# VectorE in written order around the context's last rows, and the second matrix's sums on GpSimd from the third pair on

## The chip, the core and the metric

The kernel runs on one core of a Trainium2 chip. A core has five engines that take their instructions from queues of their own: PE (TensorE, matrix products), DVE (VectorE, element-wise work), ACT (ScalarE, activations and copies), POOL (GpSimd) and SP (SyncE, which here only issues DMAs). They meet through semaphores. The metric is device time in microseconds, the median of repeated executions.

## The reference

One inference step of a layer over 1280 rows of width 1024: 1024 latent rows and 256 context rows. All of it is float32. The part that matters here is the end of the layer:

```python
x  = x + gt1 * (merged @ w_out)
u2 = rmsnorm(x, g_norm2) * (1 + sc2) + sh2
x  = x + gt2 * (jnp.square(jax.nn.relu(u2 @ w_ff1)) @ w_ff2)
y  = rmsnorm(x, g_final)
```

`w_ff1` has 4096 columns and `w_ff2` 4096 rows. The scales and shifts differ between latent and context rows.

## The kernel before

The rows lie in ten tiles of 128 rows, `xt[0..9]`, in one large buffer `z`. Three groups of rows are named `GROUPS`: two of 512 latent rows (tiles 0 to 3 and 4 to 7) and one of 256 context rows (tiles 8 and 9). Each product of float32 numbers is made of three products of rounded parts: an operand is split into a high part, which ACT rounds, and a low part, which DVE subtracts (`h` and `l` at the end of a tile's name). So each new operand needs an ACT and a DVE instruction before PE can use it all.

**The output projection** (`project_out`, L1140) makes 24 matmuls for each row tile and each block of columns, into a PSUM tile `po`. DVE multiplies it by the gate (L1153) and adds it to the row (L1155); ACT sums the squares of the row's new part into `fsq` (L1156). For the context rows it is called by `context_out(q)` in four quarters of 256 columns; each splits four tiles of weights (`raw_wc`, `hi_wc`, `lo_wc`; L861 to L864).

**The normalisation and transposition** (`modulate_ff(g)`, L1100) reduces `fsq` (L1104), makes the reciprocal root (DVE L129, then POOL L130), scales the rows by quarters of columns (`xn`; even tiles on ACT L1116, odd ones on DVE L1118), transposes them on PE (`pt`, L1124) and applies scale and shift on ACT. For latent groups the result is `u2r`, split into `u2h` and `u2l` (L1136, L1137). For the context it is split in place into `u2c` (L1129, L1130).

**The first feed-forward matrix** works on pairs of 128-column blocks, 16 pairs in all. For the latent rows it uses a scheme with seven block products instead of eight: with the four quarters B11, B12, B21, B22 of `u2` (row sums, L762) come T1 to T4, and from the weights come sums of their own (L929). `Pair.begin` makes the products with B11 and B21, `contexts` those of the context rows with `u2c` (`fc`), `rest` those with T4, T2, T3, T1 and B22 in this order. `split_sum` (L771, L772) splits the T tiles. Each product's weights are split in turn (`a_` and `s_` tiles, L854 and L855). `sums` prepares the left operands of the second matrix and stores them.

**The second matrix's sums** (`second_sums(fp)`): SP loads two 512 KB blocks of `w_ff2` into four buffers of `z` (L1221), POOL makes four subtractions (L1224), and a POOL DMA stores the result to `scr_t` (L1225). There is one set of these buffers, and it is where the context's rows `xt[8]` and `xt[9]` lie until they have been stored and scaled. The later phase that multiplies by `w_ff2` (from L1280 on) reads `scr_t`.

**The order of the work.** The kernel is written with a tile framework. Its scheduler orders each engine's instructions, by a simulated time of its own and by the order in which they are written, so an instruction that is ready early may run ahead of earlier written ones on its engine. A `Pinned` wrapper (L35) takes this freedom away: an instruction that is issued through it stays behind the one written just before it on its engine. In the kernel before, only an early phase is pinned (L258 to L395); here VectorE, GpSimd and SP are not. An engine runs its queue in order, and a waiting instruction holds up those behind it.

Around the change, the text of the kernel before has this order: `modulate_ff(1)`, `context_out(2)`, `context_out(3)`, pairs 0 and 1 `begin`, `modulate_ff(2)`, all row sums, the splits of T4, T3, T2, T1, `contexts` of pairs 0 and 1, then for each pair `rest`, `sums` and its `second_sums`.

Of the kernel before, what the change touches and what calls it, by code (L numbers as in the profile page):

```python
# [10 lines left out]
ALU = mybir.AluOpType  # L11
# [37 lines left out]
def hybrid_step(  # L49
# [6 lines left out]
    nc = tc.nc  # L56
    engines = nc.vector, nc.scalar, nc.gpsimd, nc.tensor
    V, A, G, PE = engines
    SP = nc.sync
# [9 lines left out]
    def slot(name, dt=F32R):  # L69
        return sp.tile([P, 512], dt, tag="s", name=name)  # L70
# [4 lines left out]
    def ps_mm(name):  # L75
        return pp.tile([P, 512], F32, tag="mm", name=name, bufs=3)

    def ps_sd(name):
        return pp.tile([P, 512], F32, tag="sd", name=name, bufs=5)

    def small(shape, name, bufs=4):
        return cp.tile(shape, F32, tag=f"sm{shape[-1]}", name=name, bufs=bufs)
# [44 lines left out]
    def rstd_of(ssq, n, name):  # L127
        r = small([P, 16], f"rs_{name}")
        V.tensor_scalar(r[:, :n], ssq, 1.0 / n_of[name[0]], EPS, ALU.mult, ALU.add)  # L129
        G.tensor_tensor(r[:, :n], r[:, :n], neghalf[:, :n], ALU.pow)  # L130
        return r
# [126 lines left out]
    V, A, G, PE = (Pinned(tc, e) for e in engines)  # L258
# [136 lines left out]
    V, A, G, PE = engines  # L395
# [83 lines left out]
    for g in range(3):  # L479
        t0, n = GROUPS[g]  # L480
# [168 lines left out]
    for q in range(2):  # L649
        wq = [load_w(w_sv[q, hf], f"sv{q}_{hf}", eng=G) for hf in range(2)]  # L650
        for i in range(NT):
            g, o = (i * P) // 512, (i * P) % 512
# [18 lines left out]
    def zs(i, n=1):  # L671
        return z[:, i * 512 : (i + n) * 512]
# [82 lines left out]
    def quarter_sums(raw):  # L755
        for kk in range(4):
            b11, b21, b12, b22 = raw["B11"][kk], raw["B21"][kk], raw["B12"][kk], raw["B22"][kk]
            if raw is u_raw:
                for t, k, g in ((b11, kk, 0), (b12, kk, 1), (b22, kk + 4, 1), (b21, kk + 4, 0)):
                    SP.dma_start(t, scr_u[g][k])  # L760
            for out, x, y in ((b11, b12, b11), (b12, b22, b12), (b22, b22, b11), (b21, b22, b21)):
                V.tensor_tensor(out, x, y, ALU.subtract)  # L762

    def split_sum(dst, raw, nm):
        for kk in range(4):
            t = raw[SUMS[nm]][kk]
            if nm == "T2" and kk < 3:
                hi, lo = (six(f"t2{i}{kk}") for i in "hl")
            else:
                hi, lo = slot(f"{nm}h{kk}"), slot(f"{nm}l{kk}")  # L770
            A.copy(hi, t)  # L771
            V.tensor_tensor(lo, t, hi.bitcast(F32), ALU.subtract)  # L772
            dst[nm, kk] = hi, lo
# [69 lines left out]
    def six(name):  # L843
        return q1.tile([P, 512], F32R, tag="th", name=name, bufs=6)
# [4 lines left out]
    def tmp2(name, dt=F32):  # L849
        return q1.tile([P, 512], dt, tag="s", name=name, bufs=6)  # L850
# [156 lines left out]
    for ri, r in enumerate(ORDER):  # L1007
        scr = (scr_ya, scr_yb, scr_yc)[r]
        ys = [[] for _ in range(4)]
        for g in range(3):  # L1010
            for kc in range(4):
                t0, n = GROUPS[g]
# [6 lines left out]
        for d in range(KT):  # L1019
            if d % 2 == 0:  # L1020
                wb = [load_half(w_branch[r, d // 2][:, i * 512 : i * 512 + 512], f"wb{r}_{d}_{i}") for i in range(2)]
            for g in range(3):
                t0, n = GROUPS[g]
# [45 lines left out]
    def context_weights(q):  # L1069

        src = w_out[q // 2][:, :, q % 2 * 256 : q % 2 * 256 + 256].rearrange("(j k) p c -> j p k c", k=2)
        return [load_half(src[i], f"wc{q}_{i}", lambda t: t.rearrange("p (k c) -> p k c", k=2)) for i in range(4)]
# [24 lines left out]

    fsq = cp.tile([P, NT, 4], F32, name="fsq")

    def modulate_ff(g):  # L1100
        t0, n = GROUPS[g]
        tiles = range(t0 // P, (t0 + n) // P)
        fs = small([P, 4], f"fs{g}")[:, : len(tiles)]
        V.reduce_sum(fs, fsq[:, tiles[0] : tiles[-1] + 1, 0 : 4 if g == 2 else 2], axis=mybir.AxisListType.X)  # L1104
        r = rstd_of(fs, len(tiles), f"f{g}")

        j = 1 if g == 2 else 0
        for qt in range(4):
            xn = []
            for ii, i in enumerate(tiles):  # L1110
                if ii % 2 == 0:
                    t = tmp2(f"xn{i}_{qt}")
                v = t[:, (ii % 2) * 256 : (ii % 2) * 256 + 256]
                xv = xt[i][:, qt * 256 : (qt + 1) * 256]
                if ii % 2 == 0:
                    A.activation(v, xv, AF.Copy, scale=r[:, ii : ii + 1])  # L1116
                else:
                    V.tensor_scalar(v, xv, r[:, ii : ii + 1], None, ALU.mult)  # L1118
                xn.append(v)
            for kk in range(2):  # L1120
                k = qt * 2 + kk
                ps = ps_sd(f"pt2{g}_{k}")
                for ii in range(n // P):
                    PE.transpose(ps[:, ii * P : (ii + 1) * P], xn[ii][:, kk * P : (kk + 1) * P], ident)  # L1124
                if g == 2:
                    c = slot(f"u2{k}c")
                    u2c[k] = hi, lo = c[:, 0:256], c[:, 256:512]
                    A.activation(ps[:, :n], ps[:, :n], AF.Identity, bias=sh2[:, k, j : j + 1], scale=a2[:, k, j : j + 1])
                    V.tensor_copy(hi, ps[:, :n])  # L1129
                    V.tensor_tensor(lo, ps[:, :n], hi.bitcast(F32), ALU.subtract)  # L1130
                    continue
                rf = raw2[g][k] = slot(f"u2r{k}_{g}", F32)
                A.activation(rf, ps[:, :n], AF.Identity, bias=sh2[:, k, j : j + 1], scale=a2[:, k, j : j + 1])
                if g == 0 or k >= 4:
                    hi, lo = slot(f"u2h{k}_{g}"), slot(f"u2l{k}_{g}")
                    V.tensor_copy(hi, rf)  # L1136
                    V.tensor_tensor(lo, rf, hi.bitcast(F32), ALU.subtract)  # L1137
                    u2s[f"B{1 + k // 4}{1 + g}", k % 4] = hi, lo

    def project_out(tiles, c0, n, weights):  # L1140

        for i in tiles:
            g = min(i // 4, 2)
            o = i * P - GROUPS[g][0]
            full = ps_mm(f"po{c0}_{i}")
            ps = full[:, :n]
            for k in range(KT):
                whi, wlo = weights(k)
                mh, ml = mT[k][g]
                PE.matmul(ps, mh[:, o : o + P], whi, start=k == 0, stop=False)  # L1150
                PE.matmul(ps, ml[:, o : o + P], whi, start=False, stop=False)  # L1151
                PE.matmul(ps, mh[:, o : o + P], wlo, start=False, stop=k == KT - 1)  # L1152
            V.tensor_tensor(ps, ps, gt1[(2 if g == 2 else 0) + c0 // 512][:, c0 % 512 : c0 % 512 + n], ALU.mult)  # L1153
            xc = xt[i][:, c0 : c0 + n]
            V.tensor_tensor(xc, xc, ps, ALU.add)  # L1155
            A.activation(ps, xc, AF.Square, accum_out=fsq[:, i, c0 // n : c0 // n + 1])  # L1156
            if c0 + n == D:
                SP.dma_start(scr_x[i], xt[i])

    def context_out(q):  # L1160
        ws = context_weights(q)
        project_out((8, 9), q * 256, 256, lambda k: tuple(w[:, k % 2 * 256 : k % 2 * 256 + 256] for w in ws[k // 2]))

    project_out(range(8), 0, 512, lambda k: w_out0[k])
    w_out1 = out_weights(1)
    project_out(range(5), 512, 512, lambda k: w_out1[k])
    modulate_ff(0)
    project_out(range(5, 8), 512, 512, lambda k: w_out1[k])  # L1170
    context_out(0)
    context_out(1)
    modulate_ff(1)
    quarters = (("B11", 0, 0), ("B21", 0, 4), ("B12", 1, 0), ("B22", 1, 4))
    raw2q = {nm: raw2[g][o : o + 4] for nm, g, o in quarters}
    context_out(2)
    context_out(3)

# [36 lines left out]
    def second_sums(fp):  # L1217

        q = [zs(16 + i) for i in range(4)]
        for r in range(2):  # L1220
            SP.dma_start(zs(16 + 2 * r, 2), w_ff2[2 * fp + r])  # L1221
        b11, b12, b21, b22 = q
        for out, x, y in ((b11, b12, b11), (b12, b22, b12), (b22, b22, b11), (b21, b22, b21)):
            G.tensor_tensor(out, x, y, ALU.subtract)  # L1224
        G.dma_start(scr_t[fp], zs(16, 4).rearrange("p (q c) -> p q c", c=512))  # L1225


    pairs = {}

    def feed_pair(fp):  # L1230
        odd = fp % 2
        pairs[fp] = FeedPair(
            f"{fp}", fp, (w_ff1[2 * fp], w_ff1[2 * fp + 1]), 4 if odd else 0, range(8, 12) if odd else range(12, 16), u2s, u2c)

    for fp in (0, 1):
        feed_pair(fp)
        pairs[fp].begin()
    modulate_ff(2)
    quarter_sums(raw2q)
    for nm in ("T4", "T3", "T2", "T1"):  # L1240
        split_sum(u2s, raw2q, nm)
    for fp in (0, 1):
        pairs[fp].contexts()
    for fp in range(NFP):
        if fp not in pairs:
            feed_pair(fp)
            pairs[fp].begin()
            pairs[fp].contexts()
        pairs[fp].rest()
        pairs[fp].sums()  # L1250
        del pairs[fp]
        second_sums(fp)


    pa.close()
# [261 lines left out]
```

## Time and profile before

| | |
|---|---|
| median of 3 runs | 1947.99 us (1946.2 to 1952.21) |
| profiled execution | 1952.31 us, its span 1950.5 us |
| busy share of the span: PE, DVE, ACT, POOL | 98%, 66%, 44%, 20% |
| mean granted TensorE clock | 0.996 |
| longest waits of PE from 1100 to 1260 us | 3.0, 1.5, 0.8 and 0.4 us |

How to read the rows: a row of the timeline has the start, the duration, the engine, the line, the operation, the written and the read tiles (buffer numbers left out, so all buffers of a pool share a name), and, in brackets, how long the engine stood idle before it and what ended that. Merged rows have a count (x4). A row of the windows has the stretch, its length, the busy time and number of instructions of each engine, the granted TensorE clock (1.00 is full speed), the share and rate of the DMA engines. A row of the waits has the waiting instruction, what it waited for, and the sum, number and longest of the waits.

### The profile page before, as it was taken

Reading aid. Unit: us, or ns where it says so; the run is one execution under the profiler, and the core shown is the slowest. Engines: PE = TensorE matmul, PEld = TensorE weight load, DVE = VectorE, ACT = ScalarE, POOL = GpSimd, SP = SyncE. Lnnn points to the kernel's source line nnn. Section 1 sums busy time; section 2 is a strip of 40 time slices with the busy share of each in tenths; the row PEclk is TensorE's granted clock in tenths of the full one; section 3 lists DMA queues with packets and bytes.
Section 4 is the critical chain, followed back from the end, with each engine's and each line's share of the span. In section 5 each row is a group of like instructions: output and inputs, shape, how many; then the busy total and the mean of one; then the engine's idle time right before and its main releaser. Section 6 shows DMA issues by size and latency. Waiting matters only on the chain.

```text
span 1950.5 us, 28164 instructions
## 1 busy us (share of the span) xinstructions
PE 1905.8 (98%) x10160; PEld 1628.3 (83%) x10160; DVE 1295.9 (66%) x2205; ACT 863.2 (44%) x1767; POOL 381.1 (20%) x380
## 2 busy tenths in 40 slices
PE   6999999999999999999999999999999999999998
PEld 3788888998788888888888888888888888888886
DVE  6584443347849889785665489788776655654665
ACT  7443554653233333342123375554454545443443
POOL 1200001117302424230000005445531110000003
PEclk9999999999999999999999999999999999999999
DMA  9111111012534445459533335776773596654444
GB/s 358 76 44 40 48 38 40 27 52 73 191 126 160 153 157 164 136 180 335 166 114 113 141 117 185 278 263 254 265 263 137 190 335 203 208 172 151 166 134 159
DMA packets 148989, 312.71 MB, mean 160 GB/s; under 512 B 17520, under 2 KB 40944, under 8 KB 146800
## 3 DMA queue, kind: packets, MB, share of 16 engines
q1 hardware_dynamic: 107024, 220.10, 33.8%
q0 software_dynamic: 15520, 57.75, 7.8%
q10 hardware_dynamic: 26304, 33.04, 4.7%
q8 instruction: 80, 1.31, 0.3%
q14 instruction: 61, 0.50, 0.1%
HBM read 217.47 MB, written 93.36 MB: 159 GB/s over the span
## 4 chain that ended last, share of the span: by engine, by line
PE 54%; DVE 3%; issue 1%; ACT 0%; DMA 0%; POOL 0%; ACTq 0%; POOLq 0%; DVEq 0%
PE w L1385 6%; PE w L1386 6%; PE w L1387 6%; PE fT L874 3%; PE fT L872 3%; PE fT L873 3%; PE pb L1033 3%; PE pb L1032 3%; PE pb L1034 3%; PE fB L874 2%; PE fB L872 2%; PE fB L873 2%; PE po L1152 2%; PE po L1151 2%; PE po L1150 2%; PE fc L874 1%
## 5 line engine op out<-in xcount | busy, mean ns | idle before, releaser
L1224 POOL TENSOR_TENSOR z<-z 128x512 f32<-128x512 f32 x64 | 101.5, 1586 | 128.0 <-DMA z<-in_w_ff 118.7
L929 DVE TENSOR_TENSOR z<-z 128x512 f32<-128x512 f32 x112 | 94.8, 846 | 2.5
L509 POOL PARTITION_ALL_REDUCE acc<-acc x16 | 55.0, 3472 | 187.8 <-DVE acc L503 101.1
L503 DVE SCALAR_TENSOR_TENSOR acc<-z,scond,acc 128x512 f32<-128x512 f32 x112 | 86.2, 818 | 0.0
L1339 POOL TENSOR_TENSOR rs_y<-rs_y,neghalf 128x1 f32<-128x1 f32 x10 | 9.6, 958 | 334.5 <-DVE rs_y L1338 334.4
L1190 ACT ACTIVATE z<-z 128x512 f32<-128x512 f32 x64 | 40.5, 633 | 69.9 <-DVE z L938 38.4
L954 ACT ACTIVATE z<-z 128x512 f32<-128x512 f32 x48 | 30.4, 633 | 67.8 <-DVE z L938 29.5
L130 POOL TENSOR_TENSOR rs_h<-rs_h,neghalf 128x4 f32<-128x4 f32 (+1 forms) x12 | 10.9, 910 | 202.5 <-DVE rs_h L129 202.3
L1038 DVE TENSOR_TENSOR sg<-pb,sg 128x512 f32<-128x512 f32 (+1 forms) x48 | 28.8, 601 | 26.6 <-PE pb L1034 26.5
L863 ACT CAST hi_wb<-raw_wb 128x512 fp32r<-128x512 f32 x24 | 14.8, 622 | 64.4 <-PE pb L1033 37.2
L635 DVE SCALAR_TENSOR_TENSOR yc<-th,ccol,z 128x512 f32<-128x512 f32 (+1 forms) x12 | 7.9, 660 | 50.4 <-PE th L633 50.4
L1191 ACT ACTIVATE z<-z 128x512 f32<-128x512 f32 x64 | 40.3, 630 | 1.1
L1153 DVE TENSOR_TENSOR po<-po,gt 128x512 f32<-128x512 f32 (+1 forms) x24 | 14.6, 609 | 35.5 <-PE po L1152 35.3
L1215 POOL DMA_DIRECT2D scr_s<-x x48 | 26.4, 551 | 49.5 <-DVE x L1209 44.5
L720 POOL TENSOR_TENSOR z<-z 128x1024 f32<-128x1024 f32 (+13 forms) x20 | 33.6, 1701 | 7.7 <-ACT z L704 5.4
L510 POOL TENSOR_TENSOR acc<-acc,bt 1x512 f32<-1x512 f32 x16 | 24.0, 1515 | 56.4 <-issue 56.4
L1156 ACT ACTIVATE po<-z 128x512 f32<-128x512 f32 (+1 forms) x24 | 12.7, 529 | 48.4 <-DVE z L1155 34.2
L569 DVE SCALAR_TENSOR_TENSOR z<-z,dmb,kv 128x129 f32<-128x129 f32 x56 | 16.3, 345 | 26.2 <-PE kv L558 26.1
L1039 DVE TENSOR_TENSOR z<-z,sg 128x512 f32<-128x512 f32 (+1 forms) x48 | 28.7, 601 | 1.2
L622 DVE TENSOR_TENSOR den<-den,gcol 128x2 f32<-128x2 f32 x40 | 6.3, 160 | 33.5 <-ACT den L621 32.6
L43 PE MATMUL pm<-wah,shl 128*4 128x512 f32 x32 | 13.8, 461 | 13.8 <-ACT wah L43 13.8
L130 POOL TENSOR_TENSOR rs_f<-rs_f,neghalf 128x4 f32<-128x4 f32 (+1 forms) x3 | 3.3, 1093 | 116.9 <-DVE rs_f L129 116.9
(5165 smaller groups left out, 7293.5 us busy)
## 6 DMA issues: line engine op xcount, KB each, us to landing
z<-in_w_ff SPq DMA_DIRECT2D x64, 512.0 KB, 5.4
z<-in_w_ada SPq DMA_DIRECT2D x64, 256.0 KB, 3.2
scr_t<-z POOLq DMA_DIRECT2D x16, 1024.0 KB, 4.9
z<-in_w_in SPq DMA_DIRECT2D x24, 512.0 KB, 4.3
scr_g<-z ACTq DMA_DIRECT2D x48, 256.0 KB, 2.0
sg<-scr_g SPq DMA_DIRECT2D x48, 256.0 KB, 4.6
scr_h<-z ACTq DMA_DIRECT2D x48, 256.0 KB, 4.1
scr_s<-x POOLq DMA_DIRECT2D x48, 256.0 KB, 4.5
```

Source lines behind the costliest of these rows:

```text
L503: V.scalar_tensor_tensor(acc[j], raw, scond[:, k, j : j + 1], acc[j], ALU.mult, ALU.add)
L872: PE.matmul(ps, whi[:, s], ahi, start=first and k == ks[0], stop=False)
L873: PE.matmul(ps, whi[:, s], alo, start=False, stop=False)
L874: PE.matmul(ps, wlo[:, s], ahi, start=False, stop=end and k == ks[-1])
L929: V.tensor_tensor(out, x, y, op)
L1032: PE.matmul(pb[:, :n], whi[:, s], yh, start=kc == 0, stop=False)
L1033: PE.matmul(pb[:, :n], whi[:, s], yl, start=False, stop=False)
L1034: PE.matmul(pb[:, :n], wlo[:, s], yh, start=False, stop=kc == 3)
L1224: G.tensor_tensor(out, x, y, ALU.subtract)
L1385: PE.matmul(banks[j], h_[:, s], rh, start=fp == 0, stop=False)
L1386: PE.matmul(banks[j], l_[:, s], rh, start=False, stop=False)
L1387: PE.matmul(banks[j], h_[:, s], rl, start=False, stop=fp == NFP - 1)
```

## The change

It has three parts.

1. VectorE is pinned from `context_out(2)` to `context_out(3)`, and again from `modulate_ff(2)` to the splits of the T tiles; between the two, `begin` of pairs 0 and 1 is not pinned. The row sums, 16 differences, are cut into four groups of four. One group follows `context_out(2)`; one stands in `context_out(3)` ahead of its last tile's products and addition; one stands in `modulate_ff(2)` between the request of the reciprocal root and the first scaling; one follows `modulate_ff(2)`. T2 is split ahead of T3.
2. The weights of pairs 0 and 1 are requested earlier in the text, ahead of `context_out(2)`.
3. SP is pinned in the loop over the pairs, and `second_sums` are not called for pairs 0 and 1: pair 2 and pair 3 call two each, in order, and from pair 4 on each calls one.

```diff
-    def modulate_ff(g):
+    def modulate_ff(g, between=None):
...
         r = rstd_of(fs, len(tiles), f"f{g}")
+        if between:
+            between()
...
-    def project_out(tiles, c0, n, weights):
+    def project_out(tiles, c0, n, weights, between=None):
 
         for i in tiles:
+            if between and i == tiles[-1]:
+                between()
...
-    context_out(2)
-    context_out(3)
...
     for fp in (0, 1):
         feed_pair(fp)
+
+    def row_sums(kk):
+        b11, b21, b12, b22 = (raw2q[nm][kk] for nm in ("B11", "B21", "B12", "B22"))
+        for out, x, y in ((b11, b12, b11), (b12, b22, b12), (b22, b22, b11), (b21, b22, b21)):
+            V.tensor_tensor(out, x, y, ALU.subtract)
+
+
+    V = Pinned(tc, engines[0])
+    context_out(2)
+    row_sums(0)
+    context_out(3, lambda: row_sums(1))
+    V = engines[0]
+    for fp in (0, 1):
         pairs[fp].begin()
-    modulate_ff(2)
-    quarter_sums(raw2q)
-    for nm in ("T4", "T3", "T2", "T1"):
+    V = Pinned(tc, engines[0])
+
+    modulate_ff(2, lambda: row_sums(2))
+    row_sums(3)
+    for nm in ("T4", "T2", "T3", "T1"):
         split_sum(u2s, raw2q, nm)
+    V = engines[0]
     for fp in (0, 1):
         pairs[fp].contexts()
+    SP = Pinned(tc, nc.sync)
+    summed = 0
     for fp in range(NFP):
...
         pairs[fp].sums()
         del pairs[fp]
-        second_sums(fp)
+
+        for _ in range(min(2, fp + 1 - summed) if fp > 1 else 0):
+            second_sums(summed)
+            summed += 1
+    SP = nc.sync
```

More of the change, by code (lines that the diff above doesn't have):

```diff
@@ L1158, in project_out, with context_out @@
                 SP.dma_start(scr_x[i], xt[i])
-    def context_out(q):
+    def context_out(q, between=None):
         ws = context_weights(q)
-        project_out((8, 9), q * 256, 256, lambda k: tuple(w[:, k % 2 * 256 : k % 2 * 256 + 256] for w in ws[k // 2]))
+        project_out((8, 9), q * 256, 256, lambda k: tuple(w[:, k % 2 * 256 : k % 2 * 256 + 256] for w in ws[k // 2]), between)
     project_out(range(8), 0, 512, lambda k: w_out0[k])
```

## The prediction

> **What bounds the kernel.** I read the page from the top: engines, then TensorE's (PE's) waits in the stretch that the change touches, then that stretch cut into windows, then the engines in order of time.
>
> ```profile
> PE 1905.8 (98%) x10160; PEld 1628.3 (83%) x10160; DVE 1295.9 (66%) x2205; ACT 863.2 (44%) x1767; POOL 381.1 (20%) x380
> ```
>
> TensorE is busy for 98% of the span, so a change elsewhere is worth only the PE time that it takes away or adds. From 1100 to 1260 us, which holds everything the diff touches up to the fourth pair, PE's waits are four:
>
> ```profile
> PE pt L1124 <- ACT xn L1116: 3.0, 1, 3.0
> PE fc L874 <- DVE a_0l L855: 1.5, 1, 1.5
> PE fT L874 <- DVE s_0l L855: 0.8, 1, 0.8
> PE fT L872 <- ACT a_0h L854: 0.4, 1, 0.4
> ```
>
> The windows (length, then PE, weight loads, DVE, ACT, POOL busy; then granted clock) put them in place:
>
> ```profile
> 1138.00:1164.10 26.10, 26.10 (x179) 24.00 (x178) 25.16 (x50) 18.11 (x38) 0.00 (x0) 1.00 0.19 68
> 1164.10:1176.80 12.70, 9.58 (x65) 8.88 (x64) 10.33 (x25) 10.25 (x21) 4.79 (x4) 0.87 0.35 126
> 1176.80:1190.20 13.40, 10.76 (x68) 9.31 (x68) 13.40 (x22) 10.52 (x23) 5.27 (x4) 1.00 0.53 177
> ...
> 1207.00:1560.00 353.00, 353.00 (x1872) 305.40 (x1871) 266.40 (x396) 177.85 (x330) 136.49 (x150) 1.00 0.66 235
> ```
>
> PE is full to 1164.1 and from 1207 on. Idle are 3.12 us (12.70 - 9.58) and 2.64 us (13.40 - 10.76), 5.8 together. Inside the first hole the clock also falls:
>
> ```profile
> 1164.10:1167.20 3.10, 0.14 (x1) 0.00 (x0) 2.11 (x6) 2.26 (x5) 0.70 (x1) 1.00 0.23 88
> 1167.20:1168.50 1.30, 1.22 (x6) 1.22 (x7) 0.40 (x2) 1.30 (x5) 0.00 (x0) 0.56 0.53 200
> 1168.50:1169.50 1.00, 1.00 (x7) 0.88 (x5) 0.59 (x2) 1.00 (x3) 0.00 (x0) 0.50 0.63 106
> ```
>
> From 1167.28 to about 1176.7 PE runs 16 transposes and 48 context matmuls. Full-speed prices are in these rows: 20 transposes in 2.35, and matmuls of 256 columns starting 0.12 apart.
>
> ```profile
> 1138.19 2.35 PE L1124 MATMUL pt<-cst,xn 128*128 128x128 f32 x20
> ...
> 1152.93 0.28 PE L1151 MATMUL po<-hi_wc,m7c 128*128 128x256 f32 x1
> 1153.05 0.28 PE L1152 MATMUL po<-lo_wc,m7c 128*128 128x256 f32 x1
> ```
>
> So 16 x 0.118 + 48 x 0.12 = 7.6 us of work took 9.4: 1.8 us beside the idle time. **At most 5.8 + 1.8 = 7.6 us, 0.39% of the span, can be won here.** About 0.3% (5.9 us) is what a measurement of this kernel can tell from no change.
>
> VectorE sets the holes:
>
> ```profile
> 1160.41 0.69 DVE L1137 TENSOR_TENSOR u2l<-u2r,u2h 128x512 fp32r<-128x512 f32 x1
> 1161.01 0.42 DVE L1155 TENSOR_TENSOR z<-z,po 128x256 f32<-128x256 f32 x1
> ...
> 1163.75 0.16 DVE L1104 TENSOR_REDUCE fs<-fsq 128x2 f32<-128x8 f32 x1
> ...
> 1166.46 1.14 DVE L1118 TENSOR_SCALAR xn<-z,rs_f 128x256 f32<-128x256 f32 x4 [0.81 <-POOL rs_f L130]
> ...
> 1174.23 0.42 DVE L1130 TENSOR_TENSOR u27c<-pt,u27c 128x256 fp32r<-128x256 f32 x1
> 1174.57 1.21 DVE L772 TENSOR_TENSOR T4l<-u2r,T4h 128x512 fp32r<-128x512 f32 x1
> 1175.70 1.78 DVE L855 TENSOR_TENSOR a_0l<-z,a_0h 128x512 fp32r<-128x512 f32 x1
> 1177.40 2.99 DVE L772 TENSOR_TENSOR T4l<-u2r,T4h 128x512 fp32r<-128x512 f32 x3
> 1180.31 0.68 DVE L855 TENSOR_TENSOR a_0l<-z,a_0h 128x512 fp32r<-128x512 f32 x1
> ```
>
> The last context product was done at 1153.3, but its addition ran at 1161.0, behind row sums, and the rows' reduction (call it R) at 1163.75. The last low part of the context rows (call it X) ended at 1174.65, R + 10.9. Then five instructions took 5.74 us from 1174.57 to 1180.31, where two neighbours start 0.60 apart (1160.41, 1161.01): 2.74 us lost, exactly while GpSimd subtracts:
>
> ```profile
> 1165.73 0.70 POOL L130 TENSOR_TENSOR rs_f<-rs_f,neghalf 128x2 f32<-128x2 f32 x1 [33.16 <-DVE rs_f L129]
> 1172.55 6.09 POOL L1224 TENSOR_TENSOR z<-z 128x512 f32<-128x512 f32 x4 [6.12 <-ACT pt L1128]
> 1178.93 0.62 POOL L1225 DMA_DIRECT2D scr_t<-z  x1 [0.30 <-POOL z L1224]
> 1187.30 12.79 POOL L1224 TENSOR_TENSOR z<-z 128x512 f32<-128x512 f32 x4 [7.75 <-DMA z<-in_w_ff]
> ```
>
> **Part one: additions in front of the row sums, R earlier.** From 1131 to 1163.75 VectorE had these groups:
>
> ```profile
> L762 DVE TENSOR_TENSOR u2r<-u2r,u2r 128x512 f32<-128x512 f32 x15 | 10.2, 689 | 0.0
> ...
> L772 DVE TENSOR_TENSOR t2l<-u2r,t2h 128x512 fp32r<-128x512 f32 x3 | 2.1, 691 | 0.0
> ```
>
> The new order leaves 8 of the 16 row sums in front of R instead of 15, and none of the three t2l: (7 + 3) x 0.60 = 6.0 us less, R at 1157.8 at best. Against this stands the pin. Each pinned instruction goes behind what was written before it on VectorE, so the low parts of the context weights' third quarter (four lo_wc) come behind the last u2l. ScalarE makes the rows that u2l needs:
>
> ```profile
> 1134.52 0.69 DVE L864 TENSOR_TENSOR lo_wc<-raw_wc,hi_wc 128x512 fp32r<-128x512 f32 x1
> ...
> 1138.83 0.78 ACT L1133 ACTIVATE u2r<-pt,sh,a 128x512 f32<-128x512 f32 x1 [0.21 <-PE pt L1124]
> ...
> 1143.08 1.44 ACT L1133 ACTIVATE u2r<-pt,sh,a 128x512 f32<-128x512 f32 x2
> ```
>
> Eight activations of the second group, the first at 1138.8, about 0.67 apart (two in 1.44), then a cast and a u2l of 1.0, give 1145.2 at the earliest, where the lo_wc of that quarter, by their count the third four, now begin near 1134.5. Then in written order: four lo_wc 2.4, two multiplies and additions 1.4, a row sum group 2.4, four lo_wc 2.4, one tile 0.7, a group 2.4, one tile 0.7: R = 1157.6, if PE never makes VectorE wait. If it does at each quarter, some 5 us later, 1163. I take the middle, 1160.5.
>
> **The written order inside the last rows costs time.** Before, four xn ran in one go and casts flowed from several tiles. Now each quarter's xn stands behind the low parts of the quarter in front:
>
> ```profile
> 1172.80 0.54 ACT L1128 ACTIVATE pt<-pt,sh,a 128x256 f32<-128x256 f32 x1 [0.39 <-PE pt L1124]
> ```
>
> xn 0.35, two transposes 0.4, activation 0.54, four casts and low parts at 0.33 (1174.23 to 1174.57), with handoffs 2.7 us a quarter, 10.9 in all. In front of the first xn stand the reduction and a scaling (0.3) and the third row sum group (2.4), behind which the power on GpSimd (0.70) is hidden. X = R + 13.6: 2.7 more than before. With R = 1160.5, X = 1174.1 (1171.2 to 1176.6), almost as before. The row sums have gone from in front of R to behind it.
>
> **After X.** Before, PE reached T2's product at 1190.2, X + 15.5. Now: the fourth group 2.4, four T4l 2.4, the first T2l 0.6, three differences and a split for the pair 2.4: X + 7.8, or X + 10.2 if the pairs' four low parts don't fit into VectorE's gaps of 1.4 us a quarter. PE needs 0.7 for what the last row still leaves and the window's 10.76, some of which fits into gaps ahead of X: X + 10 to X + 11.5. I take X + 11, since T2 in front of T3 is also the order in which the products use them. That is 1185.1: a gain of 5.1. I take off 1.1 for PE gaps between 1140 and 1158 (half of the 2.4 us row sum group that stands in front of the last quarter's low parts). Forecast gain 4.0; R at its ends gives 2.6 - 1.1 = 1.5 to the bound of 7.6.
>
> **Part two: the GpSimd sums.** The first two pairs' L1224, 8 instructions, leave the stretch. VectorE gets back 2.74 us; the sum above has it, through 0.60 a low part. They run in pairs two and three instead, where PE is full and VectorE has 266.4 of 353 us; a lost 2.74 us per four instructions is covered by the 6 us a pair that VectorE has free, and without that cover would be PE's.
>
> Here a rule speaks against counting on this. The Trainium skill, SBUF — State Buffer, section "Who interferes with whom", calls the port pair of VectorE and GpSimd an exclusive lock, so the moved subtractions block VectorE wherever they run. The rows agree: low parts of 1.78 instead of 0.68 beside L1224. By the rule the moved price is the same 2.7 us for every four, in a stage with room for it.
>
> **SP in written order.** Two 512 KB loads for each pair of first weights (L887) and two for each second sum (L1221) now queue as: pair 2, s0, s1, pair 3, s2, s3, pair 4, s4, pair 5, and so on. Each s load waits for the s store before it, and pairs' weights wait behind.
>
> ```profile
> 1167.67 16.26 SPq L1221 DMA_DIRECT2D z<-in_w_ff  x4
> 1192.46 3.44 SPq L887 DMA_DIRECT2D z<-in_w_ff  x2
> 1204.70 0.80 SPq L1221 DMA_DIRECT2D z<-in_w_ff  x2
> ...
> 1223.17 0.91 SPq L1221 DMA_DIRECT2D z<-in_w_ff  x2
> L872 PE MATMUL fB<-u2h,a_4h x8: 389/389/389, 1264.2 to 1268.9; 128*128 128x512 f32 x8
> z<-in_w_ff SPq DMA_DIRECT2D x64, 512.0 KB, 5.4
> ```
>
> Sums follow each other at 18.5 us (1204.70 to 1223.17) to 20.8 (1183.9, the end of the four, to 1204.70). With s0 at 1192 (where pair 2's weights go), s3 is at 1192 + 3 x 18.9 = 1248.7, pair 4's weights at 1249.7, landed 5.4 later (page, part 6) and split 1.3 later: 1256.4. PE needs them by 1264.2 at the latest, or 1260 with the gain. Price nothing, 4 us of slack; pair 3's, behind s1, has more.
>
> **Rivals.**
> - *All of it is won.* R near 1157.6, PE filled from 1140 on by the first pairs' B11 and B21 (what PE does between 1153.2 and 1164.1, 10.9 us), no wait left: gain 6.5 to 7.6, 1941. For it: those products wait for nothing of the context. Against: X = R + 13.6. Chance 0.22.
> - *Given back.* R near 1163, X two later than before, PE starved by the 2.7 us a quarter: 0 to 1.5 gain, 1947.5. For it: PE has only 2 x 0.72 us of context matmuls a quarter unless the second halves' splits are ready. Chance 0.15.
> - *Slower: pair 4's weights come late.* Each us of the sums' cycle over (1260 - 6.7 - 1 - 1192) / 3 = 20.1 costs PE three. The cycle of 20.8 was seen with L1224 at 3.2 us each beside a full VectorE. At 23, 8.7 us lost, 4 won: 1952.7. Chance 0.12.
> - *Slower: PE starves at 1141.* The pairs' splits want buffers which the context's raw and low weights now hold longer. If less than 4.9 us of B products is ready, PE waits from 1140.3 to 1145.2, and again 3.6 us until the last quarter's low parts; 8.5 in all, and 1.8 of slow clock as in the rows above, against 5.8 won: 1952.5. Chance 0.11.
> - Forecast, between these: 0.40.
>
> For the slow clock there is a rule too: the Trainium skill, TensorE: Matmul & The Clock Gate, Part 1, gives half rate after about 3.4 us of idle. This trace has 0.50 after 3.04 us of idle matmuls, so a shorter hole was enough by that row; by the rule the new order's short gaps keep the clock, by the row a gap of 3 us doesn't, and the sum would differ by 1.8.
>
> **The numbers.** The sum is made on the profiled execution, 1952.31 us with span 1950.5; it lies 4.3 above the median of 1947.99, and I take 4.0 from the median: 1944.0. The forecast's own range is 1942 to 1946.5. Through the rivals, 1939.5 to 1953. Faster by over 0.3% (below 1942.1): the first rival and an edge of the forecast, 0.26. Slower by over 0.3% (over 1953.8): a half of the two slower rivals and a twentieth from the others' far ends, since a new order on three queues can end outside what one mechanism costs, 0.16. The same: 0.58.
>
> **What will show it.** R and X on VectorE in the new trace (R earlier by 2 to 6, X about as before); xn one by one; low parts at 0.68 after X; no L1224 before pair 2; PE's waits after X under 1 us, its clock at 1.00. Wrong would be: a PE wait on lo_wc between 1140 and 1158, a wait on in_w_ff before pair 4, or X before 1171 or after 1177.

## The result, and the profile after

The changed kernel takes **1983.32 us** (median of 4 runs, 1982.03 to 1984.4) against 1950.1 for the kernel before in 4 runs (1946.2 to 1952.42): a ratio of 1.0169, 95% interval 1.0156 to 1.0183, or 33 us slower. The forecast was 1944.0, the range ended at 1953.0. The profiled execution took 1984.36 us with a span of 1982.6.

In the lists below, line numbers are those of the changed kernel; an instruction issued through the pin shows as L43, the wrapper's line. TensorE's (PE's) busy time on the page is 12.5 us more than before (1905.8), the span 32.1 more:

```profile
PE 1918.3 (97%) x10160; PEld 1635.9 (83%) x10160; DVE 1315.0 (66%) x2205; ACT 861.4 (43%) x1767; POOL 378.2 (19%) x380
```

The number of matmuls is the same, so 12.5 us are matmuls that ran slower, and the other 19.6 are idle time. Where they lie is told first by the first product of a pair's weights with u2h in the tile views (first and last start behind the durations):

```profile
L872 PE MATMUL fB<-u2h,a_3h x8: 389/389/389, 1264.3 to 1269.1; 128*128 128x512 f32 x8
...
L872 PE MATMUL fB<-u2h,a_4h x8: 389/389/389, 1296.6 to 1301.3; 128*128 128x512 f32 x8
...
L872 PE MATMUL fB<-u2h,a_15h x8: 389/389/389, 1569.0 to 1573.8; 128*128 128x512 f32 x8
```

Before, the same rows began at 1238.7, 1264.2 and 1536.8. The lag is 25.6 us at pair 3, 32.4 at pair 4 and 32.2 at pair 15: all is lost ahead of pair 4, and nothing after it. Only 0.4 of it was there when the stretch began (the reduction L1104 of the second latent group runs at 1130.71, and ran at 1130.34 before). PE's waits from 1125 to 1310 (total, times, longest):

```profile
PE po L1156 <- DVE lo_wc L43: 9.3, 2, 5.7
PE fc L872 <- ACT a_4h L854: 3.2, 1, 3.2
PE pt L1126 <- ACT xn L1118: 2.8, 1, 2.8
PE fT L872 <- ACT s_0h L854: 1.7, 3, 1.1
PE fT L874 <- DVE s_2l L855: 1.7, 1, 1.7
PE fc L872 <- DVE u26c L43: 1.0, 1, 1.0
PE fc L872 <- DVE u20c L43: 0.9, 1, 0.9
PE fc L872 <- DVE u22c L43: 0.9, 1, 0.9
PE fc L872 <- DVE u24c L43: 0.9, 1, 0.9
```

The same stretch in windows (length; PE, weight loads, DVE, ACT, POOL busy; granted clock, where 1.00 is full speed; DMA share and rate):

```profile
1142.90:1148.90 6.00, 0.34 (x4) 0.10 (x2) 4.88 (x10) 2.96 (x5) 0.00 (x0) 0.74 0.01 1
1148.90:1152.50 3.60, 3.60 (x17) 3.60 (x18) 1.73 (x3) 0.89 (x2) 0.00 (x0) 0.50 0.65 179
...
1157.00:1160.40 3.40, 0.01 (x1) 0.01 (x1) 3.30 (x6) 1.68 (x5) 0.00 (x0) 0.85 0.00 0
1160.40:1166.20 5.80, 5.80 (x27) 5.80 (x28) 4.18 (x7) 1.83 (x3) 0.00 (x0) 0.50 0.01 3
...
1179.50:1182.20 2.70, 0.01 (x1) 0.01 (x1) 2.60 (x6) 1.83 (x4) 1.07 (x1) 1.00 0.00 0
1182.20:1193.50 11.30, 9.16 (x38) 7.34 (x38) 5.52 (x14) 4.09 (x9) 0.00 (x0) 0.55 0.06 23
1193.50:1199.70 6.20, 4.19 (x26) 3.39 (x26) 4.70 (x12) 2.82 (x7) 0.00 (x0) 1.00 0.01 3
...
1283.50:1289.10 5.60, 4.89 (x18) 4.31 (x19) 5.56 (x7) 2.67 (x7) 3.06 (x3) 0.50 0.34 127
```

There are three places. **1142.9 to 1164:** PE stands still twice, and behind the holes the clock is at half, for 3.6 and 5.8 us. **1179.5 to 1199.7:** a third hole, and behind it 11.3 us at a mean clock of 0.55, with 4.15 us idle up to 1199.7 (2.14 and 2.01). **1280 to 1290:** PE waits for pair 4's weights, with half the clock behind it. VectorE's timeline shows what made the first two:

```profile
1147.53 0.69 DVE L1139 TENSOR_TENSOR u2l<-u2r,u2h 128x512 fp32r<-128x512 f32 x1
1148.14 2.49 DVE L43 TENSOR_TENSOR lo_wc<-raw_wc,hi_wc 128x512 fp32r<-128x512 f32 x4
...
1156.88 2.86 DVE L43 TENSOR_TENSOR u2r<-u2r,u2r 128x512 f32<-128x512 f32 x4
1159.65 2.49 DVE L43 TENSOR_TENSOR lo_wc<-raw_wc,hi_wc 128x512 fp32r<-128x512 f32 x4
...
1171.72 0.42 DVE L43 TENSOR_TENSOR z<-z,po 128x256 f32<-128x256 f32 x1
1174.05 0.69 DVE L909 TENSOR_TENSOR z<-z,fB 128x512 f32<-128x512 f32 x1 [1.91 <-PE fB L874]
1179.49 0.69 DVE L909 TENSOR_TENSOR z<-z,fB 128x512 f32<-128x512 f32 x1 [4.75 <-PE fB L874]
1180.09 0.15 DVE L43 TENSOR_REDUCE fs<-fsq 128x2 f32<-128x8 f32 x1
1180.36 2.86 DVE L43 TENSOR_TENSOR u2r<-u2r,u2r 128x512 f32<-128x512 f32 x4
1183.13 0.35 DVE L43 TENSOR_SCALAR xn<-z,rs_f 128x256 f32<-128x256 f32 x1
```

The third quarter's low parts begin at 1148.14, behind the last u2l, and PE waits for them from the end of its other work. The fourth quarter's begin at 1159.65, behind a group of row sums. And the context's reduction (R in the prediction), whose last input was added at 1171.72 and squared on ScalarE by 1172.7, runs at 1180.09: between them stand the two pairs' additions L909, the second of which waits 4.75 us for PE. That the reduction is behind *these* instructions is the order of the text: `begin` of the two pairs is written ahead of `modulate_ff(2)`, and the pin starts with the reduction.

Pair 4 on ScalarE and PE:

```profile
1282.89 1.14 ACT L854 CAST a_4h<-z 128x512 fp32r<-128x512 f32 x2 [7.00 <-DMA z<-in_w_ff]
...
1283.56 0.58 PE L872 MATMUL fc<-u20c,a_4h 128*128 128x256 f32 x1 [3.25 <-ACT a_4h L854]
```

### The profile page after: what moved, and what is told of

The parts are those of the page before. It is cut to its first block, busy times and chain, and to the rows that moved or that the text cites. A ratio compares the mean times of both kernels' runs of the same rounds, so it can differ in the third digit from the quotient of the medians.

```text
span 1982.6 us, 28157 instructions
## 1 busy us (share of the span) xinstructions
PE 1918.3 (97%) x10160; PEld 1635.9 (83%) x10160; DVE 1315.0 (66%) x2205; ACT 861.4 (43%) x1767; POOL 378.2 (19%) x380
## 4 chain that ended last, share of the span: by engine, by line
PE 50%; DVE 4%; DMA 2%; issue 2%; POOL 1%; ACT 1%; SPq 0%; POOLq 0%; ACTq 0%; DVEq 0%
PE w L1409 6%; PE w L1411 6%; PE w L1410 6%; PE pb L1032 3%; PE pb L1033 3%; PE pb L1034 3%; PE fT L872 2%; PE fT L873 2%; PE fT L874 2%; PE po L1156 2%; PE po L1154 2%; PE po L1155 2%; PE fB L874 2%; PE fB L873 2%; PE fB L872 2%
## 5 line engine op out<-in xcount | busy, mean ns | idle before, releaser
L1226 POOL TENSOR_TENSOR z<-z 128x512 f32<-128x512 f32 x64 | 95.2, 1487 | 91.7 <-DMA z<-in_w_ff 88.8
L929 DVE TENSOR_TENSOR z<-z 128x512 f32<-128x512 f32 x112 | 108.8, 972 | 2.5
L863 ACT CAST hi_wb<-raw_wb 128x512 fp32r<-128x512 f32 x24 | 14.7, 620 | 63.5 <-PE pb L1033 37.0
L1215 POOL DMA_DIRECT2D scr_c<-xc x16 | 11.6, 723 | 122.3 <-DVE xc L1214 117.0
```

What stands on the lines that cost most here:

```text
L929: V.tensor_tensor(out, x, y, op)
```

## The experiments

Each kernel below computes all of the reference. The letters in the expectations name theories, and each text says what its theory gives. "Before" in a ratio is the kernel before, on the same chip; its medians were 1952.36 (13 runs), 1950.57 (19 runs) and 1950.74 (22 runs) for the first four kernels, the next four and the last two.

The traces of these kernels don't start the stretch alike. At the reduction L1104 of the second latent group they are up to 4.7 us ahead of the kernel before (the traces without the third part and without the first pin) and up to 1.1 us behind it (the sums' part alone), although PE has had the same matmuls in the same order up to there. So where a time of one trace is compared with another's below, it is counted from that reduction. "The stretch" is the time from there to the first product of pair 15's weights with u2h: 406.5 us in the kernel before, 438.3 in the changed one.

No kernel takes out the second part of the change alone, or the order of T2 and T3. The second part shows nowhere in the changed kernel's trace: SP starts the loads of these weights at 1111.83, and at 1111.47 before.

### VectorE's part alone

The change without its third part: SP free, and each pair calls its own `second_sums`.

```diff
-    SP = Pinned(tc, nc.sync)
...
-        for _ in range(min(2, fp + 1 - summed) if fp > 1 else 0):
-            second_sums(summed)
-            summed += 1
-    SP = nc.sync
+        second_sums(fp)
```

> VectorE's written order alone; SP and the second sums as in the kernel before. Theory A (each of the three pins has a price of its own, read off the lag between the two traces: 15.3 us by the end of the first pairs' B products at 1179.4 against 1164.1, 7.8 more by the first T2 product at 1213.0 against 1189.9, 9.0 more by the second phase): about 1950 + 23 = 1973, the two waits on lo_wc (9.3 us) there, no late a_4h. Theory B (SP's order is what costs, VectorE's order only moves idle time): about 1950. Theory C (the parts only cost together, since the late sums meet a stage that VectorE already delays): under 1960.

Measured: 1977.02, ratio 1.0129 (1.0114 to 1.0144). The waits for lo_wc (9.3) and xn (2.8) are those of the changed kernel. VectorE's part makes some three quarters of the loss, a little more than expected.

### The sums' part alone

The kernel before with the third part only.

```diff
     for fp in (0, 1):
         pairs[fp].contexts()
+    SP = Pinned(tc, nc.sync)
+    summed = 0
     for fp in range(NFP):
...
-        second_sums(fp)
+
+        for _ in range(min(2, fp + 1 - summed) if fp > 1 else 0):
+            second_sums(summed)
+            summed += 1
+    SP = nc.sync
```

> The third part alone: SP in written order and the second sums from pair 2 on; VectorE free as before. Theory A: the weights of pair 4 still come behind the fourth sum's load, 7 to 9 us lost there, 2.7 us won because no GpSimd work stands beside the T4 low parts: about 1955, first T2 product 2 to 3 us earlier than 1189.9. Theory B: about 1980, as with the whole change. Theory C: 1946 to 1950.

Measured: 1955.79, ratio 1.0016 (1.0004 to 1.0027). PE's longest waits:

```profile
PE fc L872 <- ACT a_4h L854: 4.4, 1, 4.4
PE pt L1124 <- ACT xn L1116: 3.0, 1, 3.0
```

The waits for a_0l (1.5) and s_0l (0.8) of the kernel before are gone, so the sums' move does give VectorE its time back; the wait for pair 4's weights takes more than that. The two parts' ratios multiply to 1.0145, a little less than the whole's 1.0169. That a part of the loss needs both isn't shown: in the traces the stretch is 28.5 us longer than before with VectorE's part and 6.2 with the sums' part, 34.7 together, and 31.8 with both.

### Without the first pin

```diff
-    V = Pinned(tc, engines[0])
     context_out(2)
     row_sums(0)
     context_out(3, lambda: row_sums(1))
```

> The whole change without the first pin: the context's third and fourth quarter and two row sum groups are free on VectorE. Theory A: 15 us less than the whole change, about 1968; no wait on lo_wc; the reduction still comes behind the second pair's first addition, so at the end of the B products near 1164. Theory B: as the whole change, 1983.

Measured: 1966.09, ratio 1.0074 (1.0059 to 1.0089), with no wait for lo_wc. R comes at 1160.31, right behind L909 (1159.70), and PE still waits 2.8 for xn. This trace is 4.7 us ahead at L1104, so by the clock of the kernel before R is at 1165.0, and not at the 1160.5 that I had predicted for the changed kernel.

### Without the second pin

```diff
     for fp in (0, 1):
         pairs[fp].begin()
-    V = Pinned(tc, engines[0])

     modulate_ff(2, lambda: row_sums(2))
```

> The whole change without the second pin: statistics, context rows and T tiles are free on VectorE. Theory A: 7 to 8 us less than the whole change, about 1975; the reduction then follows the last row's squares (1172.7 in the changed trace) and not the pairs' addition (1180.1), and the scalings run ahead of the casts again; both waits on lo_wc stay. Theory B: 1983.

Measured: 1966.62, ratio 1.0071 (1.0056 to 1.0086): it gives back twice what was expected. The wait for lo_wc stays (10.8). Gone are the one for xn, the four at the quarters (0.9 to 1.0 each) and the slow clock behind them, and pair 4's weights cost 0.6. So **letting either pin go gives back about 1%** (0.95 and 0.98 of the whole's 1.69). With the third part's 0.16 this is more than the whole. The wait for pair 4's weights is counted twice in it: the third part makes it, and it falls from 3.2 to 0.6 without the second pin (without the first it stays at 3.0).

### The statistics ahead of the pairs' additions

If the reduction's place behind L909 were all that is wrong with the second pin, writing the reduction and the root (`statistics`, cut out of `modulate_ff` as a function of its own) ahead of `begin` would mend it. Both pins stay.

```diff
...
+    r2 = statistics(2)
     for fp in (0, 1):
         pairs[fp].begin()
     V = Pinned(tc, engines[0])
 
-    modulate_ff(2, lambda: row_sums(2))
+    modulate_ff(2, lambda: row_sums(2), r2)
```

> The whole change, but the context's statistics (reduction, scaling, power) are written ahead of the two pairs' first products; both pins stay. Theory D (the second pin's price is that the reduction stands behind the second pair's addition L909, 7.3 us after the last row's squares): the reduction at 1172.8 instead of 1180.1, PE's 2.8 us wait for the first scaling gone, and the half clock after it: 5 to 8 us less than the whole change, so a ratio to the kernel before of about 1.013. Theory E (the price is the scalings in written order among the casts): reduction earlier, but the whole kernel at most 2 us faster, 1.016.

Measured: 1982.75, ratio 1.0157 (1.014 to 1.0173): hardly any gain. VectorE's timeline says why:

```profile
1170.97 0.16 DVE L43 TENSOR_REDUCE fs<-fsq 128x2 f32<-128x8 f32 x1 [0.64 <-ACT po L1166]
...
1177.68 0.69 DVE L909 TENSOR_TENSOR z<-z,fB 128x512 f32<-128x512 f32 x1 [4.83 <-PE fB L874]
1178.29 2.87 DVE L43 TENSOR_TENSOR u2r<-u2r,u2r 128x512 f32<-128x512 f32 x4
1181.07 0.35 DVE L43 TENSOR_SCALAR xn<-z,rs_f 128x256 f32<-128x256 f32 x1
```

This trace is 1.6 us ahead of the changed kernel's at L1104. Beyond that, R is 7.5 us earlier (1170.97 for 1180.09), and the first xn only 0.5 (1181.07 for 1183.13). The next pinned instruction, the third group of row sums, still stands behind L909, and xn behind it. It isn't the reduction that the pin holds back but all that is written after the pairs' additions.

### The context weights' low parts free

The first pin stays for the multiplies, additions and row sums; only the eight lo_wc are let go.

```diff
     def context_out(q, between=None):
+        nonlocal V
+        pinned, V = V, engines[0]
         ws = context_weights(q)
+        V = pinned
```

> The whole change, but the eight low parts of the context's weights in its third and fourth quarter are not pinned; the gate multiplications, additions and row sums still are. Theory F (the first pin's price is these eight instructions behind the last u2l): no wait of PE on lo_wc, the first pin's whole 15 us gone, a ratio of about 1.008. Theory G (the buffers decide: raw weights and the pairs' splits share four buffers): a part of the waits stays, since the pairs' B products still can't start, 1.012 or more.

Measured: 1967.17, ratio 1.009 (1.0073 to 1.0106). No wait for lo_wc is left, R is at 1163.12 (again 1165.0 by the clock of the kernel before), and the interval overlaps with that of the kernel without the whole first pin. So the first pin's price is, as far as these runs tell, that of these eight instructions, held behind the u2l and the row sums.

### The sums' part alone, weights ahead of sums on SP

To the kernel with the sums' part alone: the next pair's weights are requested before the pair's sums.

```diff
-        if fp not in pairs:
-            feed_pair(fp)
+        if fp > 1:
+            if fp == 2:
+                feed_pair(fp)
             pairs[fp].begin()
...
         del pairs[fp]
+        if 2 < fp + 1 < NFP:
+            feed_pair(fp + 1)
```

> The third part alone, with the next pair's weights written ahead of the sums on SP, so that pair 4's weights don't queue behind the fourth sum's load. Theory A (the price of the third part is this queue): no wait for a_4h (4.4 us in the third part alone) and no half clock after it, about 8 us less than the third part alone; against the kernel before 2 to 3 us won, since no GpSimd work stands beside the T4 low parts: a ratio of 0.9985. Theory H (the sums cost wherever they run, through the port shared with VectorE): 1.000 to 1.002.

Measured: 1951.68, ratio 1.0005 (0.9995 to 1.0015). The wait for a_4h is gone, so SP's order made it. But a gain on the kernel before can't be told from nothing: the 3.0 for xn is still there.

### And eight row sums late

To that kernel: two of the four groups of row sums are held, one behind the reciprocal root and one behind the context's last low part; everything else on VectorE is free.

```diff
-    modulate_ff(2)
-    quarter_sums(raw2q)
...
+    late = Pinned(tc, engines[0])
+    row_sums(0, V)
+    row_sums(1, V)
+    modulate_ff(2, lambda: row_sums(2, late))
+    row_sums(3, late)
```

> As the run before it, and of the 16 row sums eight are held back: four behind the statistics, four behind the last context row's low part. Nothing else on VectorE is pinned. Theory I (the context's additions come late because the row sums run in front of them): reduction 3 to 4 us earlier than 1163.75, PE's 3.0 us wait for the first scaling and the half clock after it smaller: 2 to 4 us better than the run before it, a ratio of 0.997. Theory J (VectorE is full there anyway, so the sums are only moved to where the T tiles need them): no better than the run before it.

Measured: 1951.19, ratio 0.9996 (0.9987 to 1.0005). In the profile every hole is closed; the longest wait of PE is

```profile
PE pt L1126 <- DVE u20c L1132: 0.5, 1, 0.5
```

R is at 1159.57 and the last low part of the context rows, X, at 1171.08. In its trace the stretch is 3.9 us shorter than in the kernel before, the 2 to 4 us of theory I. The timed runs don't bear this out: the interval allows for 2.5 us at most, and theory I's 0.997 lies outside it.

### The same, the last rows in written order

To that kernel: the scalings and low parts of `modulate_ff(2)` through the pin too, behind the third group of row sums. The pairs' additions stay free, and PE has no hole ahead of it.

```diff
         if between:
             between()
+        kept, V = V, Pinned(tc, engines[0]) if between else V
...
+        V = kept
```

> As the kernel with eight late row sums (1951.2 of 1951, waits gone, R 1159.6, last low part of the context rows X 1170.7, so X = R + 11.1), but the last rows' scalings and low parts too in written order, behind the third group of row sums; the pairs' additions are still free. Theory K, the order inside the rows costs by itself: X = R + 16 or more (2.4 for the group of row sums, then 2.7 to 4 us a quarter, as R + 19.0 in the change without its first pin), PE waits of 0.7 to 0.9 at the quarters and for the first scaling, some 2 to 5 us slower: 1953 to 1956. Rival L, the waits came from the pairs' addition that the second pin put ahead of R: X = R + 13.6 as I predicted, no PE wait over 0.7, 1951.

Measured: 1953.43, ratio 1.0011 (1.0001 to 1.0022). R is at 1159.13, X at 1176.50: R + 17.4, where the free order has R + 11.5. PE's waits:

```profile
PE fc L872 <- DVE u24c L43: 1.2, 1, 1.2
PE fc L872 <- DVE u22c L43: 1.0, 1, 1.0
PE fc L872 <- DVE u26c L43: 1.0, 1, 1.0
PE fc L872 <- DVE u20c L43: 0.9, 1, 0.9
```

So the order inside the rows costs 4.1 us of waits by itself, without any half clock, as theory K had it; the stretch is 4.8 us longer than with the rows free, while the two kernels' timed intervals still overlap. The wait for xn, which the second pin had, is not there: here the pairs' additions don't stand ahead of R. One quarter on VectorE:

```profile
1165.96 0.34 DVE L43 TENSOR_SCALAR xn<-z,rs_f 128x256 f32<-128x256 f32 x1
1167.72 0.42 DVE L43 CAST u22c<-pt 128x256 fp32r<-128x256 f32 x1 [1.41 <-ACT pt L1132]
1168.18 0.43 DVE L43 TENSOR_TENSOR u22c<-pt,u22c 128x256 fp32r<-128x256 f32 x1
1168.52 0.41 DVE L43 CAST u23c<-pt 128x256 fp32r<-128x256 f32 x1
1168.97 0.42 DVE L43 TENSOR_TENSOR u23c<-pt,u23c 128x256 fp32r<-128x256 f32 x1
1169.31 0.34 DVE L43 TENSOR_SCALAR xn<-z,rs_f 128x256 f32<-128x256 f32 x1
```

From xn to xn are 3.35 us. On PE the transposes of that xn, which is written by 1166.30, start behind the context products:

```profile
1166.72 0.28 PE L874 MATMUL fc<-u21c,a_1l 128*128 128x256 f32 x1
1166.84 0.38 PE L1128 MATMUL pt<-cst,xn 128*128 128x128 f32 x2
```

### The late row sums alone

The kernel before with the eight late row sums only; SP and GpSimd as before.

```diff
-    modulate_ff(2)
-    quarter_sums(raw2q)
...
+    late = Pinned(tc, engines[0])
+    row_sums(0, V)
+    row_sums(1, V)
+    modulate_ff(2, lambda: row_sums(2, late))
+    row_sums(3, late)
```

> The kernel before with the late row sums alone: eight of sixteen behind the statistics and the last of the context's scalings, VectorE otherwise free, SP and GpSimd as before. Theory M, the row sums in front of R are all that the first hole is made of: R about 1160, PE's wait of 3.0 for xn gone with its half clock, the low parts of T4 still slow beside GpSimd, 2 to 4 us faster: 1947 to 1949 against 1951. Rival N, the gain goes into the next wait, the low parts behind it (a_0l 1.5 before, now 3 or more): 1951, within 0.1% of before.

Measured: 1953.49, ratio 1.0014 (1.0001 to 1.0027), not faster. The wait for xn is gone, and its place is taken by

```profile
PE fT L874 <- DVE s_0l L855: 2.4, 1, 2.4
PE fT L873 <- DVE T3l L772: 2.1, 1, 2.1
PE fT L873 <- DVE T4l L772: 1.7, 2, 1.4
```

with VectorE's low parts beside GpSimd's subtractions as slow as in the kernel before:

```profile
1182.47 6.90 POOL L1226 TENSOR_TENSOR z<-z 128x512 f32<-128x512 f32 x4 [7.29 <-DMA z<-in_w_ff]
...
1182.88 1.78 DVE L772 TENSOR_TENSOR T4l<-u2r,T4h 128x512 fp32r<-128x512 f32 x1
```

That is the mechanism of the rival N of its expectation, at a time slightly above N's: row sums behind R come to lie where VectorE is short of time anyway. Either gain, the earlier R and the free GpSimd, turns into the next wait without the other; with both the waits go, and what this is worth is too small for these runs.

## Why the prediction was wrong, step by step

**What bounds the kernel** stood: PE, at most 7.6 us to win, set by VectorE at the two holes. The kernel with the sums' part, weights ahead and two late groups closed those holes, and won 3.9 in its trace.

**The low parts of the context weights.** I had the place right: they come behind the last u2l, "1145.2 at the earliest". They came at 1148.14. The step that failed is the cover: "minus 1.1 for PE gaps between 1140 and 1158". The gaps were 9.3, so the term was sized at an eighth. The rival "PE starves at 1141" had been worked out at 8.5 of idle time and 1.8 of slow clock, and given 0.11. Its idle time was right to 0.8; the slow clock was under-counted: half of 3.6 us and of 5.8, together 4.7, so 14.0 in all. The run with those eight instructions free shows the cause. Why PE had no other work is read off the trace and wasn't tried by itself: ScalarE cast the first of the pairs' weights at 1141.50 before and casts it at 1159.62 now, while the late lo_wc still hold the context's raw weights.

**R.** Predicted 1160.5, measured 1180.09. I listed what the pin puts in front of R and named weights, multiplies, additions and row sums; I left out the one thing that waits for PE, the two pairs' additions, which are not pinned but written just ahead. This is the step that no rival had. The low parts set PE back, PE set L909 back, and L909 set R back. Of the 19.6 us, 12.2 were lost before the last row was squared (by 1172.7; by 1161.9 with the low parts free, on the clock of the kernel before), and 7.4 behind it, at L909. Letting the second pin go gave back 1%; moving the reduction alone gave back a tenth of that, so the statement holds for the whole block behind the pin, not for R only. No kernel moved the additions alone. What they cost is read from the kernel with the last rows in written order, which has no wait for xn.

**X = R + 13.6.** Measured R + 18.5 in the changed kernel, at a slow clock, and R + 17.4 with the clock at 1.00. Of the 3.8 that are not the clock, most is "2.7 us a quarter", which was 3.35 to 3.8. In the quarter shown, four casts and low parts took 1.59 (1167.72 to 1169.31) instead of 4 x 0.33, since a low part right behind its own cast starts 0.46 after it and not 0.33; and xn to the first cast took 1.76 instead of 1.29, since the next quarter's transposes queue on PE among the context products that it just released. I had counted the transposes at their own length.

**After X.** The low parts at 0.68 were right: no subtraction of GpSimd lies beside them any more, and three differences or splits follow at 0.60. But X + 11 was too short. The product that began at 1190.2 before begins at 1213.34, X + 14.8. PE had 11.9 us of work behind X, so nothing of the window's 10.76 had fitted in ahead of it, and waits of 2.8 lie in between (a_0h 0.4, s_0h 1.7, s_0l 0.7). The sum had no term for ScalarE's casts. "PE's waits after X under 1 us" was wrong as well: the longest for s_0h was 1.1, and s_2l cost 1.7.

**SP in written order.** "Price nothing, 4 us of slack" was wrong, and the rival for it (pair 4's weights late) had been given 0.12. The deadline was taken at 1264.2, the first product of a_4h with u2h. But PE first uses pair 4 in its context products: in the kernel before they start at 1254.65, before the weights' predicted 1256.4. The chain of loads itself was sized right: from pair 2's request on SP (1219.40, predicted 1192) to pair 4's cast (1282.89, predicted 1255.1) it took 63.5 us, and 63.1 had been predicted. PE waited 3.25 and 0.65 and ran at half the clock behind it (half of 4.89, 2.4): 6.3 of the 6.8 us by which the lag grows from pair 3 to pair 4. The order on SP is shown to be the cause by the kernel with the weights ahead.

**Both slower rivals came true at once**, with a third mechanism that I had not listed. For the one on pair 4 this was luck: its condition was a cycle of the sums over 20.1 us, and the groups on GpSimd start 17.4 to 17.8 apart (1226.88, 1244.27, 1262.08, 1279.80). Of the lag of 32.4 us at pair 4, 14.0 are the low parts, 6.8 pair 4, and 0.4 was there before; the other 11.2 lie at the third hole and behind it, where the second pin acts. I had put each rival against the whole gain and ended the range where one of them ends. But they hang together: all three are an instruction that waits for PE or for a DMA, ahead of a written-later one that PE needs. "What will show it" named the three right signs, a wait on lo_wc, a wait on pair 4's weights and X after 1177.

## What to carry to other kernels

Before pinning a block on an engine, write down what stands directly in front of it on the engine's queue and ask of each whether it waits for the engine that the block feeds: such a loop (PE waits for VectorE, which waits for PE) costs what no list of durations shows. Pin the work that is to be late, not the work that is to be early: eight row sums held back closed the hole that the second pin had left, though no gain in time came of it. And take a transfer's deadline from the first instruction that reads it in the trace, by searching for the tile on every engine.

## What was not expected of the hardware

**The clock falls after short holes, and stays down for about 3.4 us, or twice or three times that.** In narrow windows of the changed kernel the granted clock is 0.50 from 1145.8 to 1152.5, from 1159.5 to 1166.2, from 1183.3 to 1193.5 and from 1282.3 to 1289.1, and 1.00 between: some 6.8, 6.8, 10.2 and 6.8 us. In the kernel before it is 0.50 from 1167.4 to 1170.7. The holes were of 5.66, 3.60, 2.8 and 3.25 us, and of 3.04 in the kernel before. Where waits were 0.9 to 1.2 us, in the kernel with the last rows in written order, PE's clock stayed at 1.00. The Trainium skill, TensorE: Matmul & The Clock Gate, Part 1, gives a free-running window of about 3.4 us, both for the fall and for the way back. The lengths agree with such a window, while the fall didn't need 3.4 us of idle time: the first came 2.5 us after PE had stopped at 1143.2, and a hole of 2.8 us was enough for the third. What holes cost also differs between runs of one kernel: the twelve of the late row sums alone go from 1946.43 us at a mean clock of 0.997 to 1958.25 at 0.993.

**An instruction of VectorE that reads what the one in front of it wrote starts 0.46 us after it, where an unrelated one of the same size starts 0.33 after.** Both spacings stand in the quarter above: 1167.72 to 1168.18 is a cast and its own low part, 1168.18 to 1168.52 a low part and another tile's cast. Over sixteen instructions this is 1 us, of which a free order pays little (the kernel before has such pairs twice, at 1172.99 and 1173.78). The Trainium skill, VectorE: DVE Perf Modes, "The DRAIN you can't avoid", says that the next operation doesn't start until the pipe is empty, and that one which isn't held starts earlier. In these rows the dependent one starts 0.04 us behind the end of the one in front and the unrelated one 0.08 ahead of it. Whether this is what the page calls held, no run shows.
